# Masked softmax: later loads on GpSimd's queue in more widths and held back, SyncE's queue left with half-tile stores

The chip is one Trainium2; the kernel uses one of its cores. The metric is the device time of one execution in microseconds (us), lower is better; the median of several executions is quoted.

## The reference

```python
batch, heads, seq_q, seq_k = 16, 8, 256, 256
x        # float32 (16, 8, 256, 256)
lengths  # int32 (16,), random, 128 to 255
for b in range(batch):
    m = x[b, :, :, :lengths[b]]
    m = exp(m - max(m, axis=-1))
    result[b, :, :, :lengths[b]] = m / sum(m, axis=-1)   # the rest stays 0
```

The draw is fixed. The lengths are 188 233 229 243 195 252 for batches 0 to 5 and 165 210 222 180 209 157 159 199 214 248 for batches 6 to 15.

## The kernel before

A batch is one tile of 128 partitions with 16 rows of 256 float32 each, 16 KB per partition, 2 MB in all. There are twelve tile slots. VectorE clips the columns past the length to a large negative number, ScalarE takes the exponential with the row sum, VectorE multiplies by the inverse sum in two halves of eight rows. SyncE issues all stores, the first six loads and every later load that needs more than 208 columns. GpSimd issues the later loads that fit one of the widths 160 to 208.

```python
widths = [160, 168, 176, 184, 192, 200, 208]
...
narrow(nc.sync, 0, seq_k)                       # whole tiles, 16 KB a partition
for b in range(1, ahead):                       # ahead = 6
    narrow(nc.sync, b, seq_k)
for b in range(batch):
    nc.sync.wait_ge(s_out, b + 1)
    nc.sync.dma_start(out=out_f[b], in_=xt[:, b % slots]).then_inc(s_st[b], 16)
    n = b + ahead
    ...                                         # wait until the slot is free
        with nc.sync.If(v > widths[-1]):
            narrow(nc.sync, n, seq_k)
...
for n in range(ahead, batch):                   # on GpSimd
    ...                                         # wait until the slot is free
    pick(v, n, widths + [seq_k])                # the narrowest width that holds the length
...
mask(0)                                         # on VectorE
for b in range(batch):
    if b + 1 < batch:
        mask(b + 1)                             # waits for load b + 1
    for h in range(2):
        ...                                     # reciprocal, multiply half h of batch b
    ins.then_inc(s_out, 1)
```

Note that VectorE waits for load b + 1 before it finishes batch b.

The softmax here doesn't subtract the row's maximum and nothing guards it: scores larger than these inputs give would overflow.

## Time and profile before

| | before |
|---|---|
| median time | 160.13 us (three runs, 160.1 to 160.82) |
| profiled span | 158.5 us |
| busy: VectorE / ScalarE / GpSimd | 79% / 66% / 9% |
| DMA packets' time | 97.4% of 16 engines' span |
| bytes read and written | 30.2 and 33.6 MB |

The DMA issues of the profile's page say what each queue carries. The columns are: data, issuing engine, count, KB each, median us from issue to landing.

```profile
out_dram<-xt SPq DMA_DIRECT2D x16, 2048.0 KB, 24.3
xt<-in_x_dram SPq DMA_DIRECT2D x11, 2048.0 KB, 28.0
```

A transfer of 2 MB takes about 4.9 us when it is alone. Times of single packets come from the packet records of the trace, counted from the span's start. That it lands 24 to 28 us after its issue means that several others stand before it. The queues are full.

### The profile page before, as it was taken

The numbers are of one execution on the slowest core, as the hardware profiler recorded it, in microseconds if no ns is written. First come the engines' busy times: TensorE is split into PE (matmuls) and PEld (weight loads), VectorE is DVE, ScalarE is ACT, GpSimd is POOL, SyncE is SP. The second block draws the span as 40 slices with busy tenths as digits, with TensorE's granted clock in tenths as the row PEclk, the third lists the DMA queues.
The fourth block names the chain that finished last, engine by engine and source line by source line (L and its number), as shares of the span: only waits on it lengthen the run. The fifth ranks groups of instructions, "written<-read, shape, count | busy, mean of one in ns | idle before, by whom it ended". The sixth has DMA issues, their size and how long they took to land.

```text
span 158.5 us, 1141 instructions
## 1 busy us (share of the span) xinstructions
PE 0.2 (0%) x1; PEld 0.1 (0%) x1; DVE 125.6 (79%) x99; ACT 105.1 (66%) x514; POOL 14.5 (9%) x17
## 2 busy tenths in 40 slices
PE   0000000000000000000000000000000000000000
PEld 0000000000000000000000000000000000000000
DVE  6989799999999995932999439999999999990000
ACT  3005999999979794970697806988989798910000
POOL 7992000000002020000000000000000000000000
DMA  5999999999999999999999999999999999999991
GB/s 128 443 407 411 396 377 372 412 382 406 418 420 416 412 413 421 421 412 418 414 430 420 407 425 434 426 438 418 445 414 447 409 447 418 447 414 451 418 443 54
DMA packets 5590, 63.80 MB, mean 403 GB/s; under 512 B 514, under 2 KB 594, under 8 KB 2130
## 3 DMA queue, kind: packets, MB, share of 16 engines
q1 hardware_dynamic: 3888, 56.62, 86.0%
q0 software_dynamic: 1696, 7.14, 11.4%
q14 instruction: 4, 0.03, 0.1%
q10 hardware_dynamic: 2, 0.00, 0.0%
HBM read 30.21 MB, written 33.55 MB: 402 GB/s over the span
## 4 chain that ended last, share of the span: by engine, by line
DVE 48%; DMA 26%; issue 11%; ACT 3%; DVEq 0%; SPq 0%; POOL 0%; ACTq 0%; PE 0%; POOLq 0%
DMA xt<-in_x_dram 26%; DVE xt L208 23%; DVE xt L181 15%; DVE iota_h L156 5%; ACT xt L224 3%; DVE cap L166 2%; DVE inv_sum L206 2%; DVEq L194 0%; ACTq L224 0%; POOL iota_i L128 0%; SPq L114 0%; SPq L83 0%; DVEq L193 0%; DVE len_s L160 0%; PE len_f L145 0%
## 5 line engine op out<-in xcount | busy, mean ns | idle before, releaser
L224 ACT ACTIVATE xt<-xt x256 | 102.3, 401 | 32.7 <-DVE xt L181 32.7
L208 DVE TENSOR_TENSOR xt<-xt,inv_sum 128x2048 f32<-128x2048 f32 x32 | 73.3, 2292 | 1.1
L224 ACT ACTIVATION_READ_ACCUMULATOR xt<-xt x256 | 47.8, 187 | 0.0
L181 DVE TENSOR_TENSOR xt<-xt,cap 128x2048 f32<-128x2048 f32 x16 | 36.6, 2287 | 12.4 <-DMA xt<-in_x_dram 12.0
L91 POOL DMA_DIRECT2D xt<-in_x_dram x5 | 5.9, 1175 | 41.5 <-issue 41.5
L156 DVE TENSOR_SCALAR iota_h<-iota_i 128x256 f32<-128x256 int32 x1 | 8.0, 8030 | 1.6 <-POOL iota_i L128 1.6
L132 POOL MEMSET xt<- 128x1536 f32 x6 | 8.0, 1367 | 0.0
L206 DVE RECIPROCAL inv_sum<-row_sum 128x8 f32<-128x8 f32 x32 | 6.3, 196 | 1.3 <-ACT xt L224 1.3
L166 DVE TENSOR_SCALAR cap<-iota_h,len_s 128x256 f32<-128x256 f32 x16 | 5.7, 359 | 0.0
L217 ACT ACT_TABLE_LOAD x1 | 1.3, 1283 | 1.5 <-SPq L64 1.5
L160 DVE COPY len_s<-len_f 128x16 f32<-128x16 f32 x1 | 0.2, 175 | 0.4 <-PE len_f L145 0.4
L128 POOL IOTA iota_i<- 128x256 int32 x1 | 0.3, 331 | 0.0
L127 POOL MEMSET ones<- 1x128 bf16 x1 | 0.2, 194 | 0.5 <-SPq L64 0.5
L217 ACT ACTIVATE warm<-const-float32-0.0 128x1 f32<-128x1 f32 x1 | 0.2, 203 | 0.0
L145 PE MATMUL len_f<-len_b,ones 1*128 1x16 bf16 x1 | 0.2, 167 | 9.8 <-DVE len_b L158 9.8
L158 DVE CAST len_b<-word 1x16 bf16<-1x16 int32 x1 | 0.1, 149 | 0.0
L246 POOL MEMSET const-float32-0.0<- 128x1 f32 x1 | 0.1, 98 | 0.2 <-issue 0.2
L145 PEld LDWEIGHTS len_f<-len_b,ones 1*128 1x128 bf16 x1 | 0.1, 100 | 9.8 <-issue 9.8
L246 POOL MEMSET const-float32-1.0<- 128x1 f32 x1 | 0.1, 98 | 0.0
L246 POOL MEMSET const-bfloat16-1.0<- 128x1 bf16 x1 | 0.1, 98 | 0.0
L246 POOL MEMSET const-uint8-127<- 128x1 uint8 x1 | 0.1, 98 | 0.0
## 6 DMA issues: line engine op xcount, KB each, us to landing
out_dram<-xt SPq DMA_DIRECT2D x16, 2048.0 KB, 24.3
xt<-in_x_dram SPq DMA_DIRECT2D x11, 2048.0 KB, 28.0
xt<-in_x_dram POOLq DMA_DIRECT2D x2, 1280.0 KB, 38.7
xt<-in_x_dram POOLq DMA_DIRECT2D x1, 1600.0 KB, 37.8
xt<-in_x_dram POOLq DMA_DIRECT2D x1, 1472.0 KB, 36.7
xt<-in_x_dram POOLq DMA_DIRECT2D x1, 1344.0 KB, 20.8
word<-in_lengths_dram ACTq DMA_DIRECT2D x1, 0.1 KB
```

The lines of the kernel that those rows point to most:

```text
L91: engine.dma_start(out=xt[:, b % slots, :, :w], in_=x_f[b, :, :, :w]).then_inc(s_ld[b], 16)
L128: nc.gpsimd.iota(iota_i, pattern=[[1, seq_k]], base=0, channel_multiplier=0).then_inc(s_iota, 1)
L132: nc.gpsimd.memset(xt[:, b, :, low:], 0.0).then_inc(s_fill, 1)
L145: nc.tensor.matmul(len_f, lhsT=ones, rhs=len_b, start=True, stop=True).then_inc(s_lenf, 1)
L156: step(nc.vector.tensor_scalar(out=iota_h, in0=iota_i, scalar1=0.5, scalar2=None, op0=ALU.add))
L166: nc.vector.tensor_scalar(out=cap[:, b % 4, :], in0=iota_h, scalar1=len_s[:, b : b + 1], scalar2=-1.0e30, op0=ALU.subtract, op1=ALU.mult,)
L181: return nc.vector.tensor_tensor(out=t[:, :, lo:hi], in0=t[:, :, lo:hi], in1=cap[:, b % 4, None, lo:hi].to_broadcast([P, nt, hi - lo]), op ...
L206: step(nc.vector.reciprocal(out=inv_sum[:, b, s], in_=row_sum[:, b, s]))
L208: ins = nc.vector.tensor_tensor(out=t[:, s, :], in0=t[:, s, :], in1=inv_sum[:, b, s, None].to_broadcast([P, half, seq_k]), op=ALU.mult,)
L217: nc.scalar.activation(out=warm, in_=nc.const_aps.tensor(0.0, (P, 1), F32), func=EXP)
L224: ins = nc.scalar.activation(out=e, in_=e, func=EXP, accum_out=row_sum[:, bass.ds(i, 1), j],)
L246: nc = _bacc.Bacc("TRN2", target_bir_lowering=False, num_devices=1)
```

## The change

The intent: fewer bytes (widths up to 240), an undisturbed start (GpSimd waits until the fifth whole load has landed), no load behind a store on SyncE's queue, and stores that start as soon as half a tile is done. The cut diff:

```diff
-    widths = [160, 168, 176, 184, 192, 200, 208]
+    widths = list(range(160, 248, 8))
...
+        for b in range(batch):
+            for h in range(2):
+                s = slice(h * half, (h + 1) * half)
+                nc.sync.wait_ge(s_out, 2 * b + h + 1)
+                nc.sync.dma_start(
+                    out=out_f[b, :, s, :], in_=xt[:, b % slots, s, :]
+                ).then_inc(s_st[b], 16)
...
             if len(ws) == 1:
-                if ws[0] < seq_k:
-                    narrow(nc.gpsimd, b, ws[0])
+                load(nc.gpsimd, b, ws[0])
...
-            nc.sync.wait_ge(s_out, b + 1)
-            nc.sync.dma_start(out=out_f[b], in_=xt[:, b % slots]).then_inc(s_st[b], 16)
-            n = b + ahead
-            ...
-                with nc.sync.If(v > widths[-1]):
-                    narrow(nc.sync, n, seq_k)
...
+        nc.gpsimd.wait_ge(s_v, 1)      # VectorE's conversion before the memsets
         for b in range(ahead, slots):
             nc.gpsimd.memset(xt[:, b, :, low:], 0.0).then_inc(s_fill, 1)
         nc.gpsimd.wait_ge(s_word, 16)
+        nc.gpsimd.wait_ge(s_ld[ahead - 2], 16)
...
-            ins.then_inc(s_out, 1)     # once a batch
+                ins.then_inc(s_out, 1) # once a half
```

More of the change, by code (lines that the diff above doesn't have):

```diff
@@ L87, in length, with load @@
             )
-        def narrow(engine, b, w):
+        def load(engine, b, w):
             engine.dma_start(
@@ L93, in narrow @@
             ).then_inc(s_ld[b], 16)
+        load(nc.sync, 0, seq_k)
+        nc.scalar.dma_start(out=word64, in_=lengths[None, :]).then_inc(s_word, 16)
+        for b in range(1, ahead):
+            load(nc.sync, b, seq_k)
+        for b in range(batch):
[5 more added lines that the diff above has]
+                ).then_inc(s_st[b], 16)
+        nc.sync.wait_ge(s_st[-1], 32 * slots)
         def pick(v, b, ws):
             if len(ws) == 1:
-                if ws[0] < seq_k:
-                    narrow(nc.gpsimd, b, ws[0])
+                load(nc.gpsimd, b, ws[0])
                 return
@@ L105, in pick @@
                 pick(v, b, ws[m + 1 :])
-        narrow(nc.sync, 0, seq_k)
-        nc.scalar.dma_start(out=word64, in_=lengths[None, :]).then_inc(s_word, 16)
-        for b in range(1, ahead):
-            narrow(nc.sync, b, seq_k)
-        nc.sync.wait_ge(s_word, 16)
-        for b in range(batch):
-            nc.sync.wait_ge(s_out, b + 1)
-            nc.sync.dma_start(out=out_f[b], in_=xt[:, b % slots]).then_inc(s_st[b], 16)
-            n = b + ahead
-            if n < batch:
-                if n < slots:
-                    nc.sync.wait_ge(s_fill, n - ahead + 1)
-                else:
-                    nc.sync.wait_ge(s_st[n - slots], 16)
-                v = length(SP, n)
-                with nc.sync.If(v > widths[-1]):
-                    narrow(nc.sync, n, seq_k)
-        nc.sync.wait_ge(s_st[-1], 16 * slots)
-        nc.gpsimd.memset(ones, 1.0).then_inc(s_ones, 1)
         nc.gpsimd.iota(
@@ L130 @@
         ).then_inc(s_iota, 1)
+        nc.gpsimd.memset(ones, 1.0).then_inc(s_ones, 1)
+        nc.gpsimd.wait_ge(s_v, 1)
         for b in range(ahead, slots):
@@ L137 @@
             else:
-                nc.gpsimd.wait_ge(s_st[n - slots], 16)
-            v = length(POOL, n)
-            pick(v, n, widths + [seq_k])
+                nc.gpsimd.wait_ge(s_st[n - slots], 32)
+            pick(length(POOL, n), n, widths + [seq_k])
         nc.tensor.wait_ge(s_ones, 1)
```

## The prediction

> **What bounds the kernel now.** I read the page first: the busy shares, the DMA row of the 40 slices, the DMA queues.
>
> ```profile
> span 158.5 us, 1141 instructions
> ...
> DMA  5999999999999999999999999999999999999991
> ...
> q1 hardware_dynamic: 3888, 56.62, 86.0%
> q0 software_dynamic: 1696, 7.14, 11.4%
> ...
> HBM read 30.21 MB, written 33.55 MB: 402 GB/s over the span
> ```
>
> The DMA row is full from the second slice to the last but one, and the packets of the two queues (q1 SyncE's, q0 GpSimd's) take 97.4% of sixteen engines' span: 154.4 us. The missing 4 us are both ends: the packet records begin at 2.2 us and end at 156.8 us. No compute engine is near that (VectorE 79%). So the time is the bytes, at the rate they get, as long as nothing opens a hole. Then I read the stages in the windows view (columns: window, length, busy us and count of PE, PEld, DVE, ACT, POOL, then clock, DMA share, GB/s).
>
> ```profile
> 12.00:40.00 28.00, 0.00 (x0) 0.00 (x0) 26.16 (x23) 25.70 (x129) 0.96 (x1) 1.00 1.01 393
> 42.00:90.00 48.00, 0.00 (x0) 0.00 (x0) 39.46 (x34) 36.31 (x180) 2.30 (x2) 1.00 1.01 418
> 95.00:140.00 45.00, 0.00 (x0) 0.00 (x0) 44.55 (x37) 39.05 (x192) 0.00 (x0) 1.00 1.01 429
> ```
>
> Whole loads beside narrow loads get 393 GB/s, stores and loads beside narrow loads 418, whole tiles alone 429. The packet records say why: a 16384 byte packet takes 611 ns alone, about 674 ns when whole loads share the engines with narrow ones, about 623 ns when stores are in the mix; narrow packets of 4416 to 4800 bytes take 176 to 192 ns, some 397 GB/s over 16 engines. Last, the DMA queues of one window, and the end of the timeline on VectorE:
>
> ```profile
> DMA packets 418, 4.17 MB, mean 417 GB/s; under 512 B 16, under 2 KB 16, under 8 KB 225
> ...
> q1 hardware_dynamic: 209, 3.16, 75.9%
> q0 software_dynamic: 209, 1.00, 25.2%
> ```
>
> ```profile
> 130.31 2.28 DVE L181 TENSOR_TENSOR xt<-xt,cap 128x2048 f32<-128x2048 f32 x1
> ...
> 140.06 2.29 DVE L208 TENSOR_TENSOR xt<-xt,inv_sum 128x2048 f32<-128x2048 f32 x1
> ```
>
> From 80 to 90 us the two queues got the same number of packets, 209 each, not the same bytes. And VectorE ends at 142.4 us, 16 us before the kernel: what follows is a backlog of stores. VectorE waits for loads three times, 12.0 us in all, and that costs nothing while a backlog covers it.
>
> **What the Trainium skill says.** "DMA: Bandwidth & Descriptors", section "Queues, rings and completion order": each DMA engine goes round robin over its queues, one whole packet at a time. The trace agrees (209 against 209). The same page, "Issuing engines are not separate DMA queues": loads from another engine don't add bandwidth. Agrees: 418 GB/s with two queues, 429 with one. The same page, "SWDGE vs HWDGE vs iDMA": GpSimd's packets are preferably at most 4096 bytes. Here they are a little more (4416 to 4800): rows are added until 4096 is passed. "SBUF — State Buffer", section "Who interferes with whom": VectorE's tensor_scalar can hold the port that GpSimd uses, and whoever is second waits. Agrees: the 128x256 conversion at the start took 8.03 us, for as long as six memsets (7.96 us in the timeline), where a cap of the same size takes 0.35 us.
>
> **The change part by part.**
>
> *Widths.* The lengths of batches 6 to 15 are fixed: 165, 210, 222, 180, 209, 157, 159, 199, 214, 248. Before, five loads were narrow (168, 184, 160, 160, 200 columns) and five whole. After, 210, 222, 209 and 214 become 216, 224, 216 and 216; 248 stays whole, now from GpSimd. That is 152 columns of 8192 bytes less: 1.245 MB of 63.8, 2.0%. At 429 GB/s it is 2.9 us. But the 7.1 MB that these four still load move in 4320 or 4480 byte packets at about 400 GB/s: 17.9 us instead of 16.7, so 1.2 us come back. Net -1.7 us.
>
> *Holding the loads.* GpSimd's loads begin only when the fifth whole load has landed. Whole loads run alone, at 4.95 us each (the first two end at 8.6 and 13.6 us): the fifth ends at 28.4 us, the sixth at 33.4 us instead of 41.0. In the window from 12 to 40 us some 430 packets of q1 took some 63 ns more than alone, over 16 engines 1.7 us. This goes: -1.7 us.
>
> *Half-tile stores.* 4096 packets of 8192 bytes in place of 2048 of 16384. The only 8192 byte packets of the trace are instruction fetches, mostly 309 ns, against 305.5 for half of a whole one. Some 4 to 8 ns more each beside q0: 4096 x 6 / 16 = 1.5 us lost at most, 0.9 if only the 3.5 ns are. SyncE's issues are 0.33 us each, 32 of them, hidden.
>
> *Start.* The conversion now comes before the memsets (8 us down to about 0.4), but the memsets then stand before the caps, which are of the same kind: the first clip at about 11 us as before. No stores flow before 33 us anyway, so it is worth nothing.
>
> So the packets' work comes to: 768 whole-load packets, 30.2 us; nine narrow loads, 35.7 us (per row 2.1 ns over bytes at 26.8 bytes/ns, fitted to the four narrow sizes); the tenth load, whole, 5.0; stores 80.0. Sum 150.9 us against 154.4, plus the 3.8 us of the ends: **154.7 us of span if no hole opens**, against 158.5.
>
> **The hole I expect.** With 8192 byte store packets, the round robin gives loads 4480/(4480+8192) of the bytes, about 35%, some 145 GB/s, and stores some 265. In the kernel before whole loads shared q1 with stores in order; now all ten loads are on the small-packet side. With both queues full, from 33.6 us (28.9 issue, and 4.8 us from issue to first packet as for the first narrow load before), packets of 175 to 192 ns for loads and 314 ns for stores, less 1%, load 6 takes 9.1 us, then 12.4, 12.5, 10.3, 12.4, 9.0, 8.9, 10.7, 12.4, and the whole one 7.6 (its packets are as large as two stores'). They land at about 42.7, 55.1, 67.6, 78, 90.4, 99.4, 108.3, 119, 131.4 and 139 us. VectorE needs one each 7.35 us (22.82, 30.17, 37.5 in the timeline), 6 at 52.2, 7 at 59.5. So it waits from load 9 on: 3, 5, 1.6, 1.5, 3.3, 5 us. By these times the stores that VectorE has made stay ahead of what the queue has written: 23.1 against 20.0 MB at 108 us, 27.3 against 26.1 at 131. Hence no hole in the middle, but the last load is late: clip at 139.1 instead of 130.3 us. The backlog, some 2.3 MB, is gone by 144.3. From clip to the end of the last multiplication it took 12.04 us before (130.31 to 142.35); now about 12.2: 151.4. The last half store: 1.1 us from issue to first packet (0.95 to 2.2 at the start), 2.45 us of data, 1.6 us at the end: **156.6 us of span**. The hole is worth some 2 us of the 3.8 gained. The timed median was 1.65 us over the profiled span; so 158.2 us, and I take 158.0.
>
> **The rivals.**
> 1. *No hole:* loads get more than 35%, or the stores run dry in the middle and loads catch up. For it: total work decides, and the margin of stores at 131 us is only 1.2 MB. Then 154.7 of span, 156.3 us, -2.4%.
> 2. *The load queue becomes the bound outright:* the last load goes in 4096 byte packets (it would take 15 us rather than 7.6), or store packets cost more than 314 ns. Against it: the program keeps it as 4096 elements in a row. Then the last clip is at 144 to 146 us, and the time 163 us.
> 3. *GpSimd as the bound:* ten issues of 1.15 us and a few register loads, spread over 100 us; before, issue to issue took 1.2 us. Not likely to cost anything.
> 4. *Bytes alone:* -2.0% of 160.1 is 157.0 us. It ignores both the rate of narrow packets and the queue's order, which cancel in part.
>
> **Range and chances.** Work alone gives 156.3, the late last load 158.2; a few ns more on each store packet add 1 to 1.5 us. Below 156.9 (2% faster) it comes only when the hole stays under 0.6 us: 0.32. Slower by 2% needs rival 2: 0.05.
>
> **What would show it.** Whole loads landing by 33.5 us, and q0 idle until then. Packets of 8192 bytes at 309 to 316 ns, with equal counts on both queues from 34 us on, so loads at about 145 GB/s. VectorE waiting for loads some 15 to 20 us in all, late in the run, the last clip near 139 us. A DMA row with a dent in the last three slices, and less than 10 us from VectorE's end to the end. Wrong would be: unequal packet counts, a last clip before 135 us, or no dent.

## The result, and the profile after

The changed kernel took 158.15 us in the median (157.78 to 158.33) beside 160.46 us for the kernel before. The ratio is 0.985, with a 95% interval of 0.982 to 0.989. A ratio here is the mean time of one kernel's fast runs over that of the other's in the same rounds, so it is not quite the ratio of the medians. The interval leaves out 1.

The page of the changed kernel, the same rows as before:

```profile
span 156.3 us, 1148 instructions
...
DMA  5999999989999999999999999999999999996994
...
q1 hardware_dynamic: 5472, 46.14, 71.5%
q0 software_dynamic: 3568, 16.38, 26.0%
...
HBM read 28.97 MB, written 33.55 MB: 400 GB/s over the span
```

The read bytes fell by 1.24 MB, as worked out. The packets' time fell from 154.4 to 152.5 us (97.6% of 156.3). The DMA row now has a dent near the end (6 in the 37th slice).

The stages in the windows view (window, length, busy us and count of PE, PEld, DVE, ACT, POOL, clock, DMA share, GB/s):

```profile
12.00:33.00 21.00, 0.00 (x0) 0.00 (x0) 18.88 (x15) 20.73 (x105) 2.09 (x2) 1.00 1.00 418
35.00:90.00 55.00, 0.00 (x0) 0.00 (x0) 44.98 (x38) 41.37 (x206) 7.75 (x8) 1.00 1.02 416
90.00:135.00 45.00, 0.00 (x0) 0.00 (x0) 33.32 (x27) 27.59 (x137) 0.00 (x0) 1.00 1.02 418
135.00:148.00 13.00, 0.00 (x0) 0.00 (x0) 12.73 (x11) 11.60 (x58) 0.00 (x0) 1.00 0.90 377
```

The first stage rose from 393 to 418 GB/s, the long middle stays at 416 to 418, and the dent is the last row. The DMA queues from 50 to 60 us:

```profile
DMA packets 746, 4.21 MB, mean 421 GB/s; under 512 B 63, under 2 KB 63, under 8 KB 420
...
q1 hardware_dynamic: 373, 2.67, 64.0%
q0 software_dynamic: 373, 1.53, 38.1%
```

Again the counts are equal, 373 and 373, but now GpSimd's queue has 1.53 of 4.21 MB, 36%. Before, in the window that the prediction shows, it had 1.00 of 4.17 MB, 24%. Halving the store packets gave the loads half as much again. VectorE's waits for loads, and its timeline, where the last clip and the last multiplication stand:

```profile
DVE xt L176 <- DMA xt<-in_x_dram: 26.3, 10, 5.1
```

```profile
3.73 2.37 DVE L161 TENSOR_SCALAR cap<-iota_h,len_s 128x256 f32<-128x256 f32 x2
9.10 2.29 DVE L176 TENSOR_TENSOR xt<-xt,cap 128x2048 f32<-128x2048 f32 x1 [3.00 <-DMA xt<-in_x_dram]
...
131.10 2.29 DVE L176 TENSOR_TENSOR xt<-xt,cap 128x2048 f32<-128x2048 f32 x1 [2.86 <-DMA xt<-in_x_dram]
...
138.41 2.29 DVE L176 TENSOR_TENSOR xt<-xt,cap 128x2048 f32<-128x2048 f32 x1
...
148.17 2.29 DVE L203 TENSOR_TENSOR xt<-xt,inv_sum 128x2048 f32<-128x2048 f32 x1
```

VectorE ends at 150.5 us instead of 142.4, only 5.8 us before the span's end. So the kernel became faster while VectorE's end became later: the reserve of finished, unwritten tiles, which covered 16 us before, has been used up.

### The profile page after: what moved, and what is told of

It is laid out like the page before. It is cut to its first block, busy times and chain, and to the rows that moved or that the text cites. A ratio compares the mean times of both kernels' runs of the same rounds, so it can differ in the third digit from the quotient of the medians.

```text
span 156.3 us, 1148 instructions
## 1 busy us (share of the span) xinstructions
PE 0.2 (0%) x1; PEld 0.1 (0%) x1; DVE 120.7 (77%) x99; ACT 105.2 (67%) x514; POOL 20.0 (13%) x22
## 4 chain that ended last, share of the span: by engine, by line
DMA 30%; DVE 29%; issue 21%; another core or an unknown queue 8%; POOL 5%; SPq 1%; POOLq 1%; DVEq 0%
DMA xt<-in_x_dram 30%; DVE xt L203 16%; DVE xt L176 10%; POOL xt L127 3%; POOL xt L91 2%; DVE inv_sum L201 1%; SPq L91 1%; DVE cap L161 1%; POOLq L83 0%; POOLq L116 0%; DVEq L189 0%; DVEq L188 0%; POOLq L118 0%; SPq L252 0%
## 5 line engine op out<-in xcount | busy, mean ns | idle before, releaser
L219 ACT ACTIVATE xt<-xt x256 | 102.3, 401 | 40.7 <-DVE xt L176 40.7
L176 DVE TENSOR_TENSOR xt<-xt,cap 128x2048 f32<-128x2048 f32 x16 | 36.6, 2290 | 26.4 <-DMA xt<-in_x_dram 26.3
L91 POOL DMA_DIRECT2D xt<-in_x_dram x10 | 11.1, 1106 | 46.6 <-issue 46.6
L161 DVE TENSOR_SCALAR cap<-iota_h,len_s 128x256 f32<-128x256 f32 x16 | 7.2, 456 | 0.0
L151 DVE TENSOR_SCALAR iota_h<-iota_i 128x256 f32<-128x256 int32 x1 | 0.3, 294 | 1.4 <-POOL iota_i L121 1.4
L153 DVE CAST len_b<-word 1x16 bf16<-1x16 int32 x1 | 1.0, 1029 | 0.4 <-DMA word<-in_lengths_dram 0.4
```

The source lines that it names most:

```text
L91: engine.dma_start(out=xt[:, b % slots, :, :w], in_=x_f[b, :, :, :w]).then_inc(s_ld[b], 16)
L153: nc.vector.tensor_copy(out=len_b, in_=word[:, ::2]).then_inc(s_lenb, 1)
L161: nc.vector.tensor_scalar(out=cap[:, b % 4, :], in0=iota_h, scalar1=len_s[:, b : b + 1], scalar2=-1.0e30, op0=ALU.subtract, op1=ALU.mult,)
L176: return nc.vector.tensor_tensor(out=t[:, :, lo:hi], in0=t[:, :, lo:hi], in1=cap[:, b % 4, None, lo:hi].to_broadcast([P, nt, hi - lo]), op ...
L219: ins = nc.scalar.activation(out=e, in_=e, func=EXP, accum_out=row_sum[:, bass.ds(i, 1), j],)
```

## The experiments

Twelve kernels were run, in three groups, each group on one chip beside the kernel before. The question of the first group: is the gain only the packets' work, or does the sharing of the queues decide when loads land, and is the dent at the end worth its 2 us?

**Whole stores.** The changed kernel with one store per tile.

```diff
-            for h in range(2):
-                nc.sync.wait_ge(s_out, 2 * b + h + 1)
-                ...  # half a tile
+            nc.sync.wait_ge(s_out, 2 * b + 2)
+            nc.sync.dma_start(out=out_f[b], in_=xt[:, b % slots]).then_inc(s_st[b], 16)
...                                             # the waits for stores count 16 instead of 32
```

> The changed kernel with one store of a whole tile in place of two halves (packets of 16384 bytes again). Queue-share theory (the two queues take turns packet by packet, so the store packets' size sets when the loads land, and a late last load opens a hole at the end): loads get 4480/(4480+16384), some 21% of the bytes while stores are waiting, VectorE waits much more than the changed kernel's 26 us, no backlog of stores is left at the end, the hole grows from some 2 to some 6 to 8 us; about 162 us, or 2 to 3% slower than the changed kernel. Work-only theory (only the packets' summed time counts): 2048 fewer packets at about 3.5 ns and more over 16 engines, 0.5 to 1 us faster than the changed kernel, about 157.3 us.

Measured 161.63 us, ratio 1.008 to the kernel before. From 50 to 60 us GpSimd's queue got 0.96 of 4.21 MB in 230 of 461 packets. The direction is that of the queue share, and its size is right within a few tenths. Only VectorE's waiting was not much longer than in the changed kernel (27.9 us); but one of its waits was 12.2 us. Without half stores the rest of the change loses more than it wins.

**Quarter stores.** Each half store cut into two of four rows.

```diff
+                for g in range(2):
+                    s = slice(h * half + g * half // 2, h * half + (g + 1) * half // 2)
                     nc.sync.dma_start(
...                                             # the waits for stores count 64 instead of 32
```

> The changed kernel with each half-tile store cut into two of four rows (packets of 4096 bytes). Queue-share theory: loads get about half of the bytes (4480 against 4096), so they land early, VectorE waits for them less than 10 us in all, the backlog of stores at the end grows, the hole is gone; the packets cost about 0.9 us more: some 157.2 us, 0.5 to 1% faster than the changed kernel. Work-only theory: 4096 more packets, 0.5 to 1.5 us slower, about 159 us.

Measured 159.73 us, ratio 0.995: slower than the changed kernel. The DMA queues of this run from 50 to 60 us, and its waits:

```profile
q0 software_dynamic: 529, 2.20, 54.3%
q1 hardware_dynamic: 526, 1.93, 47.9%
```

```profile
DVE xt L177 <- DMA xt<-in_x_dram: 5.3, 2, 3.0
```

The sharing came out as expected: more than half of the bytes for the loads, no wait after the first two, VectorE done at 128.5 us, no dent. But the time went up. The packets cost 161.4 ns on average against 157.5 for half of the changed kernel's 314.9, so 8192 of them over 16 engines took 2.04 us more, and the removed dent gave back next to nothing. The queue-share theory is right about the loads and wrong about what the dent costs.

**No hold**, and **hold on the third load** instead of the fifth.

```diff
-        nc.gpsimd.wait_ge(s_ld[ahead - 2], 16)
+        # nothing, or: nc.gpsimd.wait_ge(s_ld[ahead - 4], 16)
```

> The changed kernel without the wait for the fifth whole load; the narrow loads are issued at about 10 us as before. Queue-share theory: the whole loads end at about 41 us again, at some 393 GB/s, which costs 1.7 us; but the narrow loads are some 1.5 MB ahead at that time, so the last load lands some 8 us earlier, and the hole of 2 us is gone: about 158 us, the same as the changed kernel within 0.5%, by another split. Work-only theory (the hold is a gain of 1.7 us and nothing else): 159.8 us, 1% slower.

> The changed kernel, held until the third whole load has landed instead of the fifth. Queue-share theory: narrow packets begin at about 26 us, some 0.7 MB ahead, so loads land some 5 us earlier and the hole is gone, while mixing lasts only 9 us and costs about 0.5 us: 156.7 to 157.3 us, 0.5 to 1% faster than the changed kernel and faster than no hold. Work-only theory: 0.5 us slower than the changed kernel.

Measured 158.55 us (0.989) without the hold and 158.22 us (0.987) with the earlier one. The 158 us foretold without the hold came out; the 156.7 to 157.3 us for the earlier hold did not. Both had no dent: with the earlier hold the windows view shows

```profile
138.00:148.00 10.00, 0.00 (x0) 0.00 (x0) 7.07 (x5) 4.10 (x22) 0.00 (x0) 1.00 1.01 428
```

where the changed kernel has

```profile
138.00:148.00 10.00, 0.00 (x0) 0.00 (x0) 9.76 (x9) 8.60 (x44) 0.00 (x0) 1.00 0.87 365
```

and yet its span is 156.4 us against 156.3. So 1.4 us of mean DMA time were saved (a share of 1.01 for 0.87 over 10 us) and nothing was won. The packet records tell where it went. Every store ends with one 4 byte packet on each of the 16 engines; for the last store these were written at:

```
us                      earliest engine   latest engine   span
kernel before           154.77            156.60          158.5
changed kernel          154.02            154.19          156.3
hold on the third load  152.09            154.31          156.4
no hold                 152.33            154.64          156.7
```

The engines drift apart by some 2 us, and the span ends 1.8 to 2.1 us after the latest. In the changed kernel the stores before the dent ended between 141.92 us on the earliest and 144.09 on the latest engine. The four half stores left take 2.45 us each, 9.8 in all. The latest engine had 10.1 us for them (144.09 to 154.19), so it stood idle for 0.3 us at most, while the earliest stood idle for some 2. In the second profile of the changed kernel (below) the latest engine went from 144.15 to 153.96 us, 9.81 us, with no idle time at all. The dent is idle time of the engines that were ahead, until VectorE delivers the next half tile; the one behind is still busy. Removing it leaves the one behind where it was.

The second group asks for the parts alone, with the changed kernel run again beside them.

> The changed kernel as it is, beside its parts on the same chip. Every theory: about 158.2 us, 0.985 of the kernel before.

Measured 157.84 us, ratio 0.985 (0.984 to 0.987).

**Widths alone** on the kernel before.

```diff
-    widths = [160, 168, 176, 184, 192, 200, 208]
+    widths = list(range(160, 248, 8))
```

> The kernel before with widths up to 240 and nothing else: four more loads go from SyncE's queue to GpSimd's, stores stay whole. Queue-share theory: while 16384 byte packets stand in the other queue GpSimd's loads get some 21% of the bytes, VectorE waits far more than the 12 us of before (20 to 35), and the 1.7 us of work saved are mostly lost: 159 to 160.5 us. Work-only theory: 1.7 us less, 158.6 us, with no more waiting that counts.

Measured 165.23 us, ratio 1.031: 1.2 MB fewer bytes and 4.9 us slower. The page of this run:

```profile
DMA  5999999999999999999999999999999989074994
GB/s 136 436 418 411 376 387 405 388 419 418 420 414 422 444 420 430 412 420 421 423 434 412 377 398 426 354 412 417 420 417 424 435 332 448 8 320 192 436 396 192
```

This is a real hole: in the 35th slice (139 to 143 us) the engines moved 8 GB/s, in the 37th 192. From 50 to 60 us GpSimd's nine loads got 1.01 of 4.27 MB in 225 of 455 packets. VectorE waited 25.4 us for them, more than twice as long as before, ended at 155.9 us, and no store was left to fill the end. My range of 159 to 160.5 us was too kind: I had expected a late load and not a hole of several us on all engines.

**Hold alone** on the kernel before.

```diff
         nc.gpsimd.wait_ge(s_word, 16)
+        nc.gpsimd.wait_ge(s_ld[ahead - 2], 16)
```

> The kernel before with GpSimd held for the fifth whole load and nothing else. Both theories: whole loads end at 33.5 instead of 41 us, and the faster rate of that stage is kept while a backlog of stores is left at the end: 1 to 1.7 us less, about 158.8 us. If the hold gains nothing by itself, 160.3 us.

Measured 159.19 us, ratio 0.993: 1.1 us faster, as expected at the lower end. The sixth whole load ended at 34.1 us instead of 40.7.

**Hold on the sixth load**, one load later than in the changed kernel.

```diff
-        nc.gpsimd.wait_ge(s_ld[ahead - 2], 16)
+        nc.gpsimd.wait_ge(s_ld[ahead - 1], 16)
```

> The changed kernel, held until the sixth whole load has landed, 5 us later. Theory of the slowest DMA engine (in the changed kernel the slowest of the 16 engines comes to the end of the stores at the very time when VectorE delivers the next ones, so the dent in the mean of the engines costs nothing, but there is no slack left): the loads' delay of 5 us comes through, the last clip is 4 to 5 us later and the time 161 to 163 us. Work-only theory: the same as the changed kernel, 158.2 us.

Measured 158.69 us with an unusual scatter (157.95 to 160.04), ratio 0.991. My 161 to 163 us were wrong. The loads began 6.0 us later (first packet at 41.6 instead of 35.6 us), but at 100 us they were only 0.15 MB behind. The DMA queues from 80 to 100 us show why:

```profile
q1 hardware_dynamic: 608, 4.44, 53.8%
q0 software_dynamic: 915, 3.73, 48.0%
```

The counts are no longer equal: SyncE's queue ran dry in between, since VectorE, waiting for loads, delivered fewer stores. Then the loads had the engines to themselves and caught up. A delay of the loads corrects itself in part; what is left of it cost 0.85 us at the medians.

The third group completes the combinations and tries a better version.

**Halves alone**, and **hold and halves** without the widths (the stores and the counting of halves from the diff above, put into the kernel before, the second with the hold).

> The kernel before with half-tile stores and nothing else. Queue-share theory: GpSimd's five loads get more of the engines while stores are waiting, but there are few of them and a backlog of stores covers the end before and after; the smaller packets cost 2.2 ns each (2450 ns for eight against 4864 ns for eight of 16384 bytes), 4096 of them over 16 engines 0.6 us: 160.3 to 161 us. If the halves were a gain by themselves (stores start half a tile earlier): 159.5 us or less.

> The kernel before with the hold and the half-tile stores, without the new widths. If the parts add up: 159.2 (hold alone) plus 0 to 0.6: 159.2 to 159.8 us, so that the widths are worth 1.3 to 1.9 us once the stores are halves, although alone they cost 4.9. If widths are worth nothing even then: 158 us.

Measured 162.58 us (1.013) for halves alone and 160.39 us (1.000) for hold and halves. Both expectations (160.3 to 161 us, and 159.2 to 159.8) were missed: halves cost more than the 0.6 us that I had reckoned. Of the 1.8 us between the last packets of halves alone and of the kernel before (158.40 and 156.60), about 1.1 are common to all engines (the mean of the 16 engines' last packets went from 155.37 to 156.44 us); the rest is one engine that falls back further: the spread at the end is 2.6 us.

Why one engine falls back stays open, as the records don't name the engine. Some steps of it go with instruction fetches: in the changed kernel (both profiles), with the hold on the third load and without the hold, the last engine's lag behind the median engine grew by 0.5 to 0.7 us within the one store during which an 8192 byte instruction fetch was carried (at 62.6, 62.2, 66.4 and 69.6 us). Other steps of this lag came without a fetch, so that the fetches are at most a part of the cause, and that was not tried.

**Old start.** GpSimd's memsets before VectorE's conversion again.

```diff
-        nc.gpsimd.wait_ge(s_v, 1)
...                                             # and memset(ones) before the iota again
```

> The changed kernel with GpSimd's old start order: the conversion on VectorE waits for six memsets again (8 us). All theories: the first clip at about 11 us instead of 9.1, no change of the time (157.9 us, within 0.3%), since stores are taken up only at 33 us. If the start counts, up to 2 us slower.

Measured 157.86 us, ratio 0.984: no change. The first clip was at 11.12 instead of 9.10 us. The start order is worth nothing here.

**Four whole loads.** Two loads less from SyncE, the hold on the second: the fifth load becomes 200 columns wide, the sixth stays whole and goes to GpSimd's queue.

```diff
-    ahead = min(6, batch)
+    ahead = min(4, batch)
...
-        nc.gpsimd.wait_ge(s_ld[ahead - 2], 16)
+        nc.gpsimd.wait_ge(s_ld[ahead - 3], 16)
```

> The changed kernel with four whole loads first instead of six and the hold on the second: the fifth load becomes 200 columns wide (56 columns of 8192 bytes, 0.46 MB less), the sixth stays whole but moves to GpSimd's queue. Work-only theory: 0.8 to 1 us faster than the changed kernel, 157 us. Queue-share theory: the loads are about as late as in the changed kernel or some us later, VectorE waits as much or more, and part of the gain is lost: 157.2 to 158.3 us.

Measured 157.12 us, ratio 0.980 (0.977 to 0.982): faster than the kernel before (by the study's mark of 2% it is unclear) and than the changed one, which has 0.985 on its two other chips and 157.84 us in its second run. Its page:

```profile
span 154.9 us, 1160 instructions
...
HBM read 28.51 MB, written 33.55 MB: 401 GB/s over the span
```

It reads 0.46 MB less, which at 429 GB/s is 1.07 us; its span is 1.1 and 1.4 us shorter than those of the two profiles of the changed kernel (156.0 and 156.3), its median time 0.7 us shorter than that of the second run. The dent is there as before at the end of its DMA row, if a smaller one. That the bytes alone are the cause was not tried apart from the earlier start of GpSimd's loads.

The combinations in one table, as the ratio to the kernel before. Rows with a star are made from the changed kernel, so they also have its start order and its last load on GpSimd's queue.

| widths | hold | halves | ratio |
|---|---|---|---|
| | | | 1 |
| x | | | 1.031 |
| | x | | 0.993 |
| | | x | 1.013 |
| x | x | | 1.008 * |
| x | | x | 0.989 * |
| | x | x | 1.000 |
| x | x | x | 0.985 * |

Of the parts, only the hold wins alone. Widths and halves each lose alone, and together they win: widths move work to the queue that gets too little, halves give that queue more. The start order is worth nothing (old start); the move of the last load to GpSimd's queue was not tried alone, so that a part of the starred ratios may be its.

## Why the prediction was right

The time, 158.0 us, was met within 0.2 us. The mechanism up to the last store was right too: shares by packets, late loads, a dent, the last clip at 138.41 us (139.1). The 156.6 us of span were worked out along the path from that clip, and its steps came out: VectorE ended at 150.5 us (151.4), the last half store's first packets came 1.1 to 1.2 us later (1.1), its data took 2.49 us (2.45), and the span ended 2.1 us after the last packet (1.6): 156.3.

What failed is the other side: what the kernel would take without the dent. The slowest DMA engine comes to its end at the same time as this path, which was not foreseen. So the hit is luck in part: with no late load and no dent some 158 us were measured as well (158.22 with the hold on the third load, 158.55 without the hold).

- **Packets' work.** "Sum 150.9 us". It came to 152.45. The narrow loads were right (35.65 us), the stores took 80.6, the whole loads 30.7, and I had left out the 4 byte packets and instruction fetches, 0.5 us. But where both queues are busy packets overlap, so that the shares add up to 1.02; the mean engine without a dent therefore still ended about where I had put it (in the run with the hold on the third load the mean of the engines' last packets is at 152.7 us, and the span's end lies 2.0 us after the latest: 154.7).
- **"154.7 us of span if no hole opens".** This step failed. The three runs without a hole had spans of 156.4, 156.7 and, with quarter stores and their 2.0 us more of packets, 158.2 us. I had reckoned with the mean of the engines. The end is the slowest one's, in the run with the hold on the third load 1.6 us after the mean (154.31 against 152.66).
- **"The hole is worth some 2 us of the 3.8 gained".** Wrong by the same amount, as it is the difference of 156.6 and 154.7: the dent is there, but the slowest engine hardly takes part in it. Removing it by the hold or by smaller packets gained nothing.
- **The share.** "About 35%, some 145 GB/s": 36%, 153 GB/s from 50 to 60 us. The last packets of loads 6 to 15 ended at 45.8, 57.8, 70.3, 80.5, 92.2, 100.8, 109.6, 120.1, 130.3 and 137.7 us, at first 3.1 us later than listed, 2.0 of them because the first narrow packet came at 35.6 and not at 33.6 us, at last 1.3 us earlier. (The packet times in the prediction, as the 2.2 and 156.8 us of its ends, lie some 0.24 us late against the span's start; differences between them hold.)
- **Waiting.** 26.3 us, but 5.3 of them are the first two loads, which had no wait before; late in the run it was 21.0, near the 15 to 20 foretold.
- **Start.** "The first clip at about 11 us as before": it was 9.10, as the two caps got through between memsets (2.37 us for both). That it is worth nothing was right (old start).
- **Widths, hold, halves.** Net -1.7, -1.7 and +0.9 to 1.5 us as separate terms. Alone they measure +4.9, -1.1 and +2.1 us. The sum was usable only because the three come together; with hold and halves in place the widths, with the last load's move, are worth 1.5% (0.985 against 1.000), 2.4 us, and not 1.7. Two workings were off: the sum of 150.9 takes the stores at 80.0 us, only 0.3 more than 2048 packets of 623 ns before, so the 0.9 to 1.5 us for halves are not in it; and the window from 12 to 40 us has 530 whole-load packets (597 records of q1 with the small ones) and not 430, with some 62 ns more each, which makes 2.1 us and not 1.7.
- **Rival 2**, the load queue as the bound, did not happen here but is what widths alone and whole stores show.

## What to carry to other kernels

When two queues are full, as here, the size of the packets in each decides who gets the bytes (GpSimd's loads got 23, 36 and 53% beside store packets of 16384, 8192 and 4096 bytes): look at the packet counts and bytes per queue before moving loads from one to the other, and cut the larger packets before giving the other queue more work. A dent in the mean of the DMA engines is no loss while the slowest engine is still busy; compare the earliest and the latest engine's last packet before spending effort on it. A change of several parts can be worth more than its parts, so a part that loses alone isn't thereby refuted.

## What the Trainium skill lacked or had wrong

- "DMA: Bandwidth & Descriptors", section "Issuing engines are not separate DMA queues": issuing from several engines is said to save sequencer time alone. It also sets how the bandwidth is shared, which follows from the turns by packet that the page tells elsewhere but isn't drawn there: GpSimd's loads got 20 to 24% of the bytes beside 16384 byte store packets, 36% beside 8192 and 53% beside 4096. Moving four loads to that queue with nothing else made the kernel 3.1% slower, with fewer bytes.
- The same page, "SWDGE vs HWDGE vs iDMA": packets of at most 4096 bytes preferably. The rows here (640 to 896 bytes) were gathered until 4096 was passed: 4320 to 4800 bytes. The last load, with whole rows, went in packets of 16384 bytes on the same queue.
- The same page's specifications give about 1 us to the first byte on GpSimd's path. From the start of the issue to the first packet it was 4.6 to 5.7 us here, with SyncE's queue full.
- "SBUF — State Buffer", "Who interferes with whom": the one that issues first holds the shared port for its instruction. How the turn passes between instructions in a row is not said: behind six memsets the conversion waited for all of them (8.03 us), while in the changed kernel two caps took 2.37 us in the middle of the same six.
- "DMA: Bandwidth & Descriptors", "Latency and other measured facts": two engines are said to be usually slower, with no size and a cause that is called a guess. No page has how far the engines drift apart in a long run: the last packets of the 16 engines lay 1.8 us apart in the kernel before, 2.2 and 2.3 in two versions without a dent, 2.6 with half stores alone, and 0.2 and 0.5 after a dent. Whether it was those two engines here the records can't say.
